# A two-layer hybrid encoder in fp32: bank layout of the prompt's Fourier mixing, and the engine that makes the weights' low parts

## The chip, the cores and the metric

The kernel runs on one core of a Trainium2 chip. The metric is the device time of one execution in microseconds; the number that counts is the median over runs. One launch computes both outputs.

## The reference

The same two layers and the same weights are applied to a prompt of 512 tokens and to a sample of 1024 tokens, all fp32, width 1024.

```python
for i in range(2):
    hn = rmsnorm(h, ln1[i])
    q, k, v, ga, uf, gf, mga, mgf = split(hn @ w_in[i])            # 1024 -> 4352 = 34 * 128
    a = band_attention(rope(q), rope(k), v, sink[i]) * silu(ga)    # 8 heads of 64, |i-j| <= 128
    f = fourier_mix(uf, w_fmix[i]) * silu(gf)
    merged = sigmoid(mga) * (a @ w_ao[i]) + sigmoid(mgf) * (f @ w_fo[i])
    h = h + merged @ w_out[i]
    gate = sigmoid(rmsnorm(h, ln_pg[i]) @ w_pg[i])
    h = h + (p[i] @ w_pe[i]) * gate
return rmsnorm(h, ln_f)

def fourier_mix(u, w):            # 4 channel groups of 128
    ug = u.reshape(B, S, 4, 128)
    f = real(fft2(ug, axes=(positions, group channels), norm="ortho"))
    return einsum("bsgc,gcd->bsgd", f, w)
```

## The kernel before

**Number format.** Every fp32 product is made of three products in fp32r. Each operand is split in two: ScalarE rounds it to the high part (L86, a cast), and the engine that `hi_lo` is given, VectorE (`V`) or GpSimd (`G`), subtracts it from the source for the low part (L87). `mm3` and `mm3_steps` then issue high by high (L98), high by low (L99) and low by high (L100) into one bank. So L86 and L87 occur all over the trace, and their groups are told apart by tile and shape.

**Stages of a layer.** The prompt is chunk 0, the sample chunks 1 and 2. `embed` (L625) makes `p @ w_pe` for all chunks. `project_prompt` (L489) multiplies the prompt by 34 weight tiles of 128 columns, 24 matmuls of 512 columns each; beside it `run` (L923) steps, at a rate written in the program, through the prompt's attention, `fourier(l, 0)` and the preparation of the sample. `project_pair` (L503) projects the sample in products of block sums (class `Pair`, matmuls on L233) beside the sample's attention. `merge(l, (0,), ...)` is the prompt's merge (branch outputs, output projection, gates), beside `fourier(l, 1)` for the sample; `merge(l, PAIR, ...)` is the sample's.

**Weights.** Class `Weights` (L148) holds a list of weight tiles. Each `get` hands out tile i, loads tile i + 3 from memory by the SyncE queue, and splits tile i + 2 in two halves of 128 x 512: `split` (L160) casts on ScalarE and subtracts on the engines in `engs`. The projection of layer 0's prompt has a list of its own, with both low parts on VectorE. From the sample's projection on, one list per layer serves everything (`streams(l)`): tiles 0 to 23 are the prompt's merge (8 for the branches, 8 output, 8 gates), the next 24 the sample's merge (16 and 8); behind these, in layer 0, stand the 34 tiles of layer 1's prompt projection, and in layer 1 the 8 gate tiles a second time, for chunk 2. All their low parts are GpSimd's.

**The prompt's Fourier part.** `fourier(l, 0)` folds the 512 positions of a channel group into two sets of 256 (`fold`, L790 on), for cosine and sine. For each set, and for even and odd positions apart, it multiplies by the channel transform (two matmuls, L854 of 256 columns and L855 of 128), into one bank each: misc, o, misc, misc. ScalarE copies one half of a bank to SBUF (L858), VectorE adds the other (L859), and the result is split again (L86, L87, 256 columns). One small product for the middle position takes an o bank. Then four sums over positions, of 128 columns (L98 to L100 into sc, sc, misc and misc), which a dozen small instructions of VectorE and ScalarE put together.

**Banks.** The eight banks of PSUM are pools: three mm, two sc, one o, two misc (`PS_BUFS`). Attention uses sc, o and misc; the norm's sums (L328) and its scale, transposed (L347 copies it out), use misc; projections and the prompt's merge use mm.

**What sets the order.** Each engine works its own instructions in the order of the program, and that order is not the one in which the source issues them: the program is built with a scheduler that simulates a timeline, so every edit moves instructions on all engines. `split` gives its tile's copies, and the release of a tile or a bank decides when the next one may be written.

**The end of a merge.** The sums of squares (L322, L323) go to TensorE (L328); the inverse root is twelve small VectorE steps (L332 to L339); TensorE transposes it, L347 copies it out, and L585 multiplies the first gate product by it and so empties its bank. With three mm banks TensorE can make three gate products before L585 has to be done.

## Time and profile before

| what | value |
|---|---|
| median of 3 runs | 2255.76 us (2255.22 to 2256.32) |
| the profiled execution, its own time | 2258.37 us |
| span of the profiled execution | 2255.9 us |
| mean granted clock of TensorE | 0.986 of full speed |
| TensorE, matmuls (PE) | 2182.3 us busy, 97% |
| VectorE (DVE) | 1460.9 us busy, 65% |
| ScalarE (ACT) | 1088.5 us busy, 48% |
| GpSimd (POOL) | 558.0 us busy, 25% |
| L87 on GpSimd, 128 x 512 | 284 instructions, 1448 ns each |
| L87 on VectorE, 128 x 512, from act | 290 instructions, 763 ns each |

All times are microseconds from the start of the span unless they say ns. A line number stands for a line of the kernel before. In the timeline, a bracket holds the idle time of the engine before the row, and the instruction that ended it; such a time is the gap between two busy times, and since matmuls overlap and their ends are modelled, starts are surer than ends. A granted clock of 1.00 is 2.4 GHz, one of 0.50 is 1.2 GHz. Names behind an operation are pools: `act` and `scr` in SBUF, `mm`, `sc`, `o` and `misc` in PSUM.

### The profile page before, as it was taken

Reading aid. Unit: us, or ns where it says so; the run is one execution under the profiler, and the core shown is the slowest. Engines: PE = TensorE matmul, PEld = TensorE weight load, DVE = VectorE, ACT = ScalarE, POOL = GpSimd, SP = SyncE. Lnnn points to the kernel's source line nnn. Section 1 sums busy time; section 2 is a strip of 40 time slices with the busy share of each in tenths; the row PEclk is TensorE's granted clock in tenths of the full one; section 3 lists DMA queues with packets and bytes.
Section 4 is the critical chain, followed back from the end, with each engine's and each line's share of the span. In section 5 each row is a group of like instructions: output and inputs, shape, how many; then the busy total and the mean of one; then the engine's idle time right before and its main releaser. Section 6 shows DMA issues by size and latency. Waiting matters only on the chain. (4 is left out here: it accounts for less than half of the span.)

```text
span 2255.9 us, 30026 instructions
## 1 busy us (share of the span) xinstructions
PE 2182.3 (97%) x10176; PEld 1809.5 (80%) x10176; DVE 1460.9 (65%) x2703; ACT 1088.5 (48%) x2340; POOL 558.0 (25%) x399
## 2 busy tenths in 40 slices
PE   8899999999999989999999999999999999999996
PEld 7777777788888878888888778787888888788885
DVE  5866657677667775464557564756766676864466
ACT  5477433466665454223324854336666644512342
POOL 0201100000004553312524253100000145641181
PEclk9899999999999999999999999999999999999998
DMA  7655544445448564731445554444444574653232
GB/s 279 230 181 167 188 140 163 148 137 166 150 133 294 189 236 174 251 103 51 146 158 188 173 178 167 151 165 137 143 141 158 194 270 159 225 201 117 83 118 98
DMA packets 240537, 380.69 MB, mean 169 GB/s; under 512 B 21120, under 2 KB 95488, under 8 KB 240384
## 3 DMA queue, kind: packets, MB, share of 16 engines
q1 hardware_dynamic: 233472, 366.19, 48.0%
q10 hardware_dynamic: 6912, 12.59, 1.5%
q8 instruction: 80, 1.31, 0.2%
q14 instruction: 73, 0.60, 0.1%
HBM read 270.17 MB, written 108.53 MB: 168 GB/s over the span
## 5 line engine op out<-in xcount | busy, mean ns | idle before, releaser
L233 PE MATMUL mm<-act,act 128*128 128x512 f32 x2856 | 695.2, 394 | 10.8 <-DVE scr L250 6.4
L233 PEld LDWEIGHTS mm<-act,act 128*128 128x128 f32 x2856 | 531.7, 188 | 123.4 <-issue 8.0
L98 PE MATMUL mm<-act,act 128*128 128x512 f32 x1408 | 559.1, 397 | 19.8 <-DVE scr L585 7.6
L100 PE MATMUL mm<-act,act 128*128 128x512 f32 x1408 | 556.5, 396 | 2.7 <-POOL act L87 1.3
L99 PE MATMUL mm<-act,act 128*128 128x512 f32 x1408 | 555.3, 394 | 0.0
L87 POOL TENSOR_TENSOR act<-act,act 128x512 fp32r<-128x512 f32 x284 | 404.1, 1448 | 547.2 <-ACT act L86 481.2
L86 ACT CAST act<-act 128x512 fp32r<-128x512 f32 x574 | 330.3, 619 | 225.1 <-DMA act<-in_w_af 60.7
L98 PEld LDWEIGHTS mm<-act,act 128*128 128x128 f32 x1408 | 267.8, 190 | 73.7 <-ACT act L86 13.0
L100 PEld LDWEIGHTS mm<-act,act 128*128 128x128 f32 x1408 | 267.5, 190 | 60.6 <-DVE act L87 3.5
L99 PEld LDWEIGHTS mm<-act,act 128*128 128x128 f32 x1408 | 268.1, 190 | 53.3
L87 DVE TENSOR_TENSOR act<-act,act 128x512 fp32r<-128x512 f32 x290 | 212.1, 763 | 47.1 <-ACT act L86 45.9
L87 DVE TENSOR_TENSOR act<-scr,act 128x512 fp32r<-128x512 f32 x256 | 193.7, 777 | 58.0 <-ACT act L86 56.3
L748 POOL TENSOR_TENSOR scr<-scr,scr 128x512 f32<-128x512 f32 x24 | 33.5, 1396 | 768.5 <-DVE scr L745 767.1
L86 ACT CAST act<-scr 128x512 fp32r<-128x512 f32 (+1 forms) x260 | 152.8, 615 | 144.4 <-DVE scr L410 69.0
L322 ACT ACTIVATE scr<-act 128x512 f32<-128x512 f32 x105 | 65.1, 631 | 233.7 <-DVE act L569 145.9
L87 DVE TENSOR_TENSOR act<-misc,act 128x512 fp32r<-128x512 f32 x132 | 88.1, 686 | 75.5 <-ACT act L86 75.1
L707 DVE CUSTOM_DVE_ANT_0 act<-sc,mask_sb,nsink_sb 128x384 f32<-128x384 f32 (+1 forms) x192 | 104.0, 569 | 46.4 <-PE sc L699 43.3
L710 ACT ACTIVATE act<-act,stat 128x385 f32<-128x385 f32 (+1 forms) x192 | 110.5, 578 | 43.9 <-DVE stat L707 43.4
L86 ACT CAST act<-misc 128x512 fp32r<-128x512 f32 x132 | 73.8, 586 | 106.8 <-PE misc L734 104.9
L98 PE MATMUL sc<-act,act 128*128 128x512 f32 (+1 forms) x292 | 111.1, 381 | 0.0
L100 PE MATMUL sc<-act,act 128*128 128x512 f32 (+1 forms) x292 | 110.6, 379 | 0.0
L99 PE MATMUL sc<-act,act 128*128 128x512 f32 (+1 forms) x292 | 110.5, 379 | 0.0
(207 smaller groups left out, 2642.8 us busy)
## 6 DMA issues: line engine op xcount, KB each, us to landing
act<-in_w_in SPq DMA_DIRECT2D x136, 256.0 KB, 4.5
act<-in_w_in SPq DMA_DIRECT2D x68, 512.0 KB, 4.8
gt<-scr SPq DMA_DIRECT2D x96, 256.0 KB, 2.3
scr<-gt SPq DMA_DIRECT2D x96, 256.0 KB, 5.3
act<-in_w_pg SPq DMA_DIRECT2D x80, 256.0 KB, 3.8
act<-in_w_af SPq DMA_DIRECT2D x64, 256.0 KB, 5.3
act<-in_w_out SPq DMA_DIRECT2D x64, 256.0 KB, 5.4
pl<-scr ACTq DMA_DIRECT2D x48, 256.0 KB, 2.5
```

The lines of the kernel that those rows point to most:

```text
L86: S.copy(hi, src)
L87: lo_eng.tensor_tensor(lo, src, f(hi), op=ALU.subtract)
L98: PE.matmul(out, wh, xh, start=i == 0, stop=False)
L99: PE.matmul(out, wh, xl, start=False, stop=False)
L100: PE.matmul(out, wl, xh, start=False, stop=i == n - 1)
L233: PE.matmul(bank, w, v, start=first and k == 0 and n == 0, stop=k == 3 and n == 2, skip_group_check=True)
L322: S.activation(sq, h, AF.Square)
L707: V.tensor_tensor_reduce(out=pr[:, :W], in0=sc[:, :W], in1=msk, scale=-0.125, scalar=nsink_sb[:, l, head : head + 1], op0=ALU.add, op1=ALU ...
L710: S.activation(pr, pr, AF.Exp, bias=nmx[:, e], scale=-1.0, accum_out=rs[:, e])
L748: G.tensor_tensor(a2, a2, gate, op=ALU.mult)
```

## The change

Three edits:

1. `split` picks its engines by the tile's number: tiles 0 to 23 of a layer's list and all from tile 48 on have both low parts on VectorE, tiles 24 to 47 stay with GpSimd. Layer 0's own projection list stays on VectorE throughout.
2. `embed` makes its first two halves of weights with a low part on VectorE, too, not on GpSimd.
3. `fourier(l, 0)`, the prompt's (s = 0), puts the sums of even and odd positions side by side in one misc bank, and one copy and one add empty it at 256 columns; the four sums go into two sc banks, two in each. The sample's Fourier part (s = 1) keeps its layout.

```diff
 # class Weights, split
-                for r, eng in zip((slice(0, 4), slice(4, 8)), self.engs):
+                for r, eng in zip((slice(0, 4), slice(4, 8)), self.engs[min(i // 24, 2)]):

 # embed
-                ws[k, i] = halves(raws[k][:, i, :], V if k else G)
+                ws[k, i] = halves(raws[k][:, i, :], V)

 # fourier: position sums of one channel group
                 for par in range(2):
-                    pm = pst(("misc", "o", "misc")[(2 * i + par) % 3])
+
+                    if s or par == 0:
+                        pm = pst(("misc", "o", "misc")[(2 * i + par) % 3] if s else "misc")
                     for t in range(n):
-                        j, lo = 2 * t * P, 2 * t * P + par
+                        j, lo = (2 * t if s else 2 * par) * P, 2 * t * P + par
                         uh, ul = (z[:, lo : lo + 2 * P - 1 : 2] for z in us[i])
                         PE.matmul(pm[:, j : j + 2 * P], uh, cw[i][:, :, gs], start=True, stop=False)
                         PE.matmul(pm[:, j : j + P], ul, cw[i][:, 0, gs], start=False, stop=True)
-                    pv = pm[:, : 2 * n * P].rearrange("p (t h d) -> p t h d", t=n, h=2)
-                    av = a[:, par * n * P : (par + 1) * n * P].rearrange("p (t d) -> p t d", t=n)
+                    if s == 0 and par == 0:
+                        continue
+                    pv = pm.rearrange("p (t h d) -> p t h d", t=2, h=2)
+                    av = (a[:, par * n * P : (par + 1) * n * P] if s else a).rearrange("p (t d) -> p t d", t=2)
                     S.copy(av, pv[:, :, 1])
                     V.tensor_tensor(av, av, pv[:, :, 0], op=ALU.add)

 # fourier: the four sums of one channel group
-            acc = [pst("sc"), pst("sc"), pst("misc"), pst("misc")]
+            if s:
+                acc = [pst("sc"), pst("sc"), pst("misc"), pst("misc")]
+            else:
+                b0, b1 = pst("sc"), pst("sc")
+                acc = [b0, b0[:, 2 * P :], b1, b1[:, 2 * P :]]

 # the program
-    ws = Weights(w_ins(0), (V, V))
+    ws = Weights(w_ins(0), ((V, V),) * 3)
...
-        ws = Weights(streams(l) + ([] if last else w_ins(l + 1)), (G, G))
+        ws = Weights(streams(l) + ([] if last else w_ins(l + 1)), ((V, V), (G, G), (V, V)))
```

In all 184 instructions move from GpSimd to VectorE, and 16 copies of ScalarE and 16 adds of VectorE go. The order on the engines changes with it, at two places above all. (Lines of the changed kernel are shifted: L856 there is L854 before, L857 is L855.)

TensorE, layer 0, the second channel group: before, from its third bank of position sums on, with the change from inside the block of both its banks on (misc and o are the position sums and the middle position, mm the projection, sc the four sums). Before:

```order
L854 MATMUL misc_2231<-act_1990,scr_2134 128x256
L855 MATMUL misc_2231<-act_1990,scr_2134 128x128
L98 MATMUL mm_2396<-act_462,act_2197 128x512
L99 MATMUL mm_2396<-act_462,act_2197 128x512
L100 MATMUL mm_2396<-act_462,act_2197 128x512
L98 MATMUL o_2251<-tiny_2137,act_1989 128x2
L99 MATMUL o_2251<-tiny_2137,act_1989 128x2
L100 MATMUL o_2251<-tiny_2137,act_1989 128x2
L854 MATMUL misc_2236<-act_1990,scr_2134 128x256
L855 MATMUL misc_2236<-act_1990,scr_2134 128x128
L98 MATMUL sc_2283<-act_1995,scr_2227 128x128
L99 MATMUL sc_2283<-act_1995,scr_2227 128x128
```

With the change:

```order
L100 MATMUL sc_2135<-act_1995,scr_2102 128x128
L98 MATMUL mm_2374<-act_344,act_2186 128x512
L857 MATMUL misc_2203<-act_1989,scr_2125 128x128
L856 MATMUL misc_2203<-act_1989,scr_2125 128x256
L857 MATMUL misc_2203<-act_1989,scr_2125 128x128
L857 MATMUL misc_2220<-act_1990,scr_2128 128x128
L856 MATMUL misc_2220<-act_1990,scr_2128 128x256
L857 MATMUL misc_2220<-act_1990,scr_2128 128x128
L99 MATMUL mm_2374<-act_344,act_2186 128x512
L100 MATMUL mm_2374<-act_344,act_2186 128x512
L98 MATMUL mm_2374<-act_358,act_2186 128x512
L99 MATMUL mm_2374<-act_358,act_2186 128x512
```

Before, the sums of the second set stood in pairs between the projection's matmuls, and the four sums followed the last pair at once. Now both sets stand in one block, with one bank for each set, and the projection's matmuls follow: 23 of them until the four sums (sc) begin.

VectorE, end of the prompt's merge in layer 0, from within the root steps (L337 to L339) to the first gate product (L585; L87 are low parts, from scr of the sample's merge, from act of weights and of the prompt). Before:

```order
L339 SCALAR_TENSOR_TENSOR tiny_7884<-misc_7879,tiny_7884 128x4
L337 TENSOR_TENSOR misc_7879<-misc_7879,tiny_7884 128x4
L338 SCALAR_TENSOR_TENSOR misc_7879<-misc_7879,tiny_7884 128x4
L339 SCALAR_TENSOR_TENSOR tiny_7884<-misc_7879,tiny_7884 128x4
L87 TENSOR_TENSOR act_7906<-act_7865,act_7906 128x512
L87 TENSOR_TENSOR act_7912<-act_7865,act_7912 128x512
L87 TENSOR_TENSOR act_7981<-scr_7915,act_7981 128x512
L87 TENSOR_TENSOR act_7986<-scr_7939,act_7986 128x512
L347 COPY scr_7960<-misc_7955 128x512
L585 TENSOR_TENSOR scr_7963<-mm_7843,scr_7960 128x512
L87 TENSOR_TENSOR act_8013<-scr_7941,act_8013 128x512
L587 SCALAR_TENSOR_TENSOR scr_7963<-scr_7963,scr_7962 128x512
```

With the change:

```order
L339 SCALAR_TENSOR_TENSOR tiny_7852<-misc_7847,tiny_7852 128x4
L87 TENSOR_TENSOR act_7874<-act_7833,act_7874 128x512
L87 TENSOR_TENSOR act_7877<-act_7827,act_7877 128x512
L87 TENSOR_TENSOR act_7880<-act_7833,act_7880 128x512
L87 TENSOR_TENSOR act_7888<-act_7802,act_7888 128x512
L87 TENSOR_TENSOR act_7891<-act_7802,act_7891 128x512
L87 TENSOR_TENSOR act_7949<-scr_7883,act_7949 128x512
L347 COPY scr_7928<-misc_7923 128x512
L87 TENSOR_TENSOR act_7954<-scr_7907,act_7954 128x512
L87 TENSOR_TENSOR act_7962<-act_7885,act_7962 128x512
L87 TENSOR_TENSOR act_7965<-act_7885,act_7965 128x512
L585 TENSOR_TENSOR scr_7931<-mm_7811,scr_7928 128x512
```

Among the steps ahead of L585 more low parts stand than before, since those of the weights are on this engine now.

## Rows read from the trace of the kernel before

**Rows 1.** Page, section 1: busy time, share of the span, instructions of each engine

```profile
PE 2182.3 (97%) x10176; PEld 1809.5 (80%) x10176; DVE 1460.9 (65%) x2703; ACT 1088.5 (48%) x2340; POOL 558.0 (25%) x399
```

**Rows 2.** Windows: stretch, us, PE, PEld, DVE, ACT, POOL busy, clock, DMA, GB/s

```profile
101.50:111.70 10.20, 6.54 (x15) 4.70 (x16) 9.45 (x16) 5.40 (x10) 0.00 (x0) 0.50 0.68 206
234.60:241.40 6.80, 6.80 (x24) 6.12 (x25) 4.56 (x23) 3.25 (x12) 0.59 (x1) 0.50 0.31 112
700.00:835.00 135.00, 129.34 (x664) 110.17 (x662) 102.42 (x184) 64.35 (x135) 78.53 (x55) 0.99 0.67 241
831.90:838.70 6.80, 3.46 (x8) 2.81 (x9) 5.88 (x9) 1.89 (x3) 1.32 (x1) 0.50 0.11 42
1200.00:1400.00 200.00, 192.57 (x930) 159.63 (x929) 115.00 (x256) 116.35 (x293) 85.74 (x64) 0.98 0.51 168
1340.50:1347.30 6.80, 6.36 (x17) 5.18 (x18) 3.31 (x15) 2.09 (x8) 2.07 (x3) 0.50 0.20 74
2000.00:2050.00 50.00, 50.00 (x222) 41.42 (x221) 25.22 (x35) 9.32 (x16) 10.59 (x8) 1.00 0.51 175
2197.20:2200.60 3.40, 3.40 (x9) 2.66 (x9) 1.50 (x13) 0.00 (x0) 0.00 (x0) 0.50 0.00 0
```

**Rows 3.** Timeline of TensorE, layer 0 Fourier; in brackets idle time before, releaser

```profile
214.49 0.39 PE L854 MATMUL misc<-act,scr 128*128 128x256 f32 x1 [0.93 <-DVE act L87]
...
224.52 0.39 PE L854 MATMUL o<-act,scr 128*128 128x256 f32 x1 [0.59 <-ACT scr L86]
...
234.60 0.58 PE L854 MATMUL misc<-act,scr 128*128 128x256 f32 x1 [2.76 <-DVE scr L859]
```

**Rows 4.** Timeline of TensorE, the prompt's Fourier part of layer 1

```profile
1319.27 0.39 PE L854 MATMUL misc<-act,scr 128*128 128x256 f32 x1 [0.93 <-DVE act L87]
...
1329.25 0.33 PE L855 MATMUL o<-act,scr 128*128 128x128 f32 x1 [0.66 <-DVE scr L87]
...
1339.23 0.33 PE L98 MATMUL misc<-act,scr 128*128 128x128 f32 x1 [1.11 <-ACT scr L86]
...
1340.94 0.69 PE L100 MATMUL misc<-act,scr 128*128 128x128 f32 x2 [1.06 <-DVE scr L87]
```

**Rows 5.** Timeline of VectorE, GpSimd and TensorE, end of the prompt's merge, layer 0

```profile
818.80 1.89 DVE L87 TENSOR_TENSOR act<-scr,act 128x512 fp32r<-128x512 f32 x3
...
820.30 12.91 POOL L87 TENSOR_TENSOR act<-act,act 128x512 fp32r<-128x512 f32 x8 [4.70 <-issue]
...
822.31 0.16 DVE L332 TENSOR_SCALAR misc<-misc 128x4 f32<-128x4 f32 x1
...
830.35 3.41 DVE L87 TENSOR_TENSOR act<-scr,act 128x512 fp32r<-128x512 f32 x2
...
834.40 0.69 DVE L585 TENSOR_TENSOR scr<-mm,scr 128x512 f32<-128x512 f32 x1
...
835.24 0.77 PE L98 MATMUL mm<-act,act 128*128 128x512 f32 x1 [5.90 <-DVE scr L585]
```

**Rows 6.** Groups by line and form: L86, L859, L858 at 256 columns

```profile
L86 ACT CAST scr<-scr 128x256 fp32r<-128x256 f32 x32 | 12.2, 405 | 17.0 <-DVE scr L859 9.8 <-DVE tiny L801 5.7 <-POOL scr L790 1.5
...
L859 DVE TENSOR_TENSOR scr<-scr,misc 128x256 f32<-128x256 f32 x24 | 9.6, 413 | 5.4 <-ACT scr L858 5.3
...
L858 ACT COPY scr<-misc 128x256 f32<-128x256 f32 x24 | 8.9, 372 | 33.6 <-PE misc L855 33.6
```

**Rows 7.** L87 on GpSimd, 1190 to 1400: ns least/median/most, and who waited

```profile
L87 POOL TENSOR_TENSOR act<-act,act x54: 1261/1297/1745, 1193.6 to 1388.8; 128x512 fp32r<-128x512 f32 x54
...
  PE mm L100: 1.3, 2
```

**Rows 8.** Timeline of TensorE, the prompt's projection in layer 0

```profile
104.04 0.76 PE L98 MATMUL mm<-act,act 128*128 128x512 f32 x1 [4.58 <-DVE scr L455]
...
106.35 0.80 PE L100 MATMUL mm<-act,act 128*128 128x512 f32 x1 [1.12 <-DVE act L87]
```

**Rows 9.** Timeline of TensorE, the last norm's sums in layer 1

```profile
2194.47 1.92 PE L328 MATMUL misc<-mean_sb,scr 128*128 128x1 f32 x16 [1.39 <-DVE scr L323]
```

## The prediction

> **What bounds the kernel now.** I read the page first, then the windows by stage, then the timeline of the engine that binds. TensorE is busy for 97% of the span [rows 1], so only two things can be won: stretches in which TensorE stands idle, and stretches in which it runs at half clock. The windows show the second [rows 2]: the granted clock is 0.50, the lower of the two levels (1.2 GHz), for 6.8 us at 234.6, 6.8 us at 831.9, 6.8 us at 1340.5 and 3.4 us at 2197.2; elsewhere, as at 2000, it is 1.00 and 222 matmuls pass in 50 us, 0.225 us each. A stretch of 6.8 us at half clock does the work of 3.4 us, so each such stretch costs at most 3.4 us.
>
> The timeline of TensorE shows what stands before each of these drops. In layer 0 the prompt's Fourier part stalls TensorE for 0.93, 0.59 and 2.76 us, and the clock falls at the end of the last stall [rows 3]. In layer 1 the same part stalls it for 0.93, 0.66, 1.11 and 1.06 us (two shorter ones are not counted), and the clock falls at 1340.5, between the last two [rows 4]. At the end of the prompt's merge in layer 0 it stands for 5.90 us [rows 5], and the clock falls within that. All of these end with VectorE or ScalarE: a bank that has not been emptied, or a low part that has not been made.
>
> Why VectorE is late there is in the same rows. While GpSimd works through eight low parts in 12.91 us, two of VectorE's own take 3.41 us; when GpSimd was idle for most of the time, three took 1.89 us, 0.63 each [rows 5]. So a low part of GpSimd's does not come free: it holds up VectorE by about 1.1 us (3.41/2 - 0.63), which is more than VectorE would need to do that low part itself.
>
> **The change, part by part.**
>
> *A. Prompt's Fourier part, layer 0.* A channel group took four banks for the position sums (three misc, one o) and four for the four sums (two sc, two misc). It now takes two misc and two sc; o is left to the middle position alone. The 2.76 us stall is the third misc bank of a group, waiting for the first to be emptied by L859; the 0.59 one waits for a high part, with TensorE already at an o bank of the next group. The order shows the new run: all eight matmuls of the position sums stand together, and 23 matmuls of the projection (5.2 us) stand before the sums that use them. That is longer than the chain they wait for: copy 0.37, add 0.41, high part 0.41, and a low part that I price as the add, 1.6 us together [rows 6]. I let 0.59 and 2.76 go: 3.3 us. The 0.93 us stall waits for a low part of the weight table (L87) and stays. The half-clock stretch follows an idle TensorE; without the stall I take it to go as well, 3.4 us (bounds 0 and 3.4). The matmuls are the same in number and shape. Sixteen copies and sixteen adds fewer in both layers together lie on ScalarE and VectorE, beside TensorE's work: nothing on the path.
>
> *B. The same in layer 1.* Of 0.93, 0.66, 1.11 and 1.06 us the first stays, 2.8 us go. Here GpSimd leaves as well: of its low parts between 1190 and 1400, 54 in all [rows 7], only the few before the next layer's weights remain. The half clock at 1340.5: 3.4 us, same bounds.
>
> *C. End of the prompt's merge, layer 0.* TensorE's fourth gate product needs the bank that L585 empties, and L585 waits for the norm's chain, which started at 822.31 with L332 and ended with L585 at 835.09: 12.8 us [rows 5]. In the new order eleven low parts stand in that chain instead of six, because the weights' come to VectorE, but GpSimd has none of its own there. Eleven at 0.63, twelve short steps at 0.16, the copy L347 and L585 at 0.69 each: 10.2 us, 2.6 less. Three matmuls fewer stand between the norm's sums and the transposes (0.7 us), so TensorE arrives sooner and gains 1.9 us of the 5.90. Bounds: 0, if ScalarE's high parts are late, and 5.90. About 4 us of idle time remain, longer than the 2.76 in A before which the clock fell, so I leave the half clock in place. In layer 1 the chain has few low parts and TensorE's own transposes set it: nothing.
>
> *D. The whole merge as a load.* Between 700 and 835 VectorE is busy for 102.4 of 135 us and GpSimd for 78.5 [rows 2]. Of the 55 instructions of GpSimd some 40 move, 25 us at 0.63; they give back up to 1.1 each where they collided. VectorE does not become the bound: at most 128 of 135 us even if nothing came back.
>
> *E. Layer 1's projection.* Its 34 weight tiles move as well, 68 low parts, since every tile from the 48th of a stream on is VectorE's. TensorE's waits for GpSimd there, 1.3 us [rows 7], go. Against this VectorE gets up to 54 x 0.63 = 34 us more in 200 us of which 115 are busy [rows 2]. Layer 0 already works in this way, and there TensorE lost 4.58 and 1.12 us to VectorE's backlog [rows 8], and 10.2 us at half clock [rows 2], 5.1 lost: 10.8 together. In layer 0 that followed two norm copies and twelve pinned products in one block; in layer 1's new order these are spread between products. I charge 2.2 us, nearer to nothing (bounds 0 and 10.8).
>
> *F. The last gates.* 16 low parts move to VectorE, whose steps were held up. The last norm's sums waited 1.39 us for L323 [rows 9], and 3.4 us at half clock followed [rows 2], 1.7 lost: 3.1 us go (bounds 0 and 3.1).
>
> *G. New stalls in the Fourier part.* Eight groups get a new order, and its gaps come out on the chip, not on paper. Bounds: nothing, and one stall like the 1.11 in each group, 8.9 us. I charge 3.0, since most places have over 20 matmuls of cover. The two low parts of the first weights go to VectorE, where it was idle. No DMA is added, removed or moved past another queue's.
>
> Sum: 3.3 + 3.4 + 2.8 + 3.4 + 1.9 + 1.3 + 3.1 = 19.2, less 2.2 and 3.0: **14.0 us**. The sum is made in the profiled execution of 2258.4 us, 2.6 us above the median of the runs, 2255.8; taken from the median it gives **2241.8 us**.
>
> *A rule against the change.* A bank with two sums can be emptied only when both are done; before, the copy of the even half could start while TensorE wrote the odd half in another bank. The Trainium skill ("PSUM — Partial Sum Buffer", Summary: rules for kernel authors) says that whoever reads a bank during matmuls should have them write a different bank. No row of this trace shows two halves in one bank. By the rule the overlap is lost; by the order TensorE has other work meanwhile, so the sum stands.
>
> **Rivals.**
>
> 1. *The half clock stays* in A, B and F, because the stretches have small matmuls enough to bring it about without a stall. For it: at 1340.5 the stalls beside it are short. Against: elsewhere the same small matmuls run at full clock. 8.5 us less gained: 2250.3.
>
> 2. *VectorE's backlog moves into layer 1's projection* as in layer 0, 10.8 instead of 2.2: 2250.4, and up to 2255 if the Fourier part behind it stalls too. For it: the same lines wait in layer 0. Against: 115 of 200 us leave room.
>
> 3. *Slower: the shared bank serialises.* If TensorE stands through the chain of 1.6 us after each of the 16 shared banks of position sums (eight groups, two each), that is 25.6 us, in place of today's 8.0 us of stalls; the half clock stays, and only C, E and F (6.3) help: 2255.8 + 25.6 - 8.0 - 6.3 = 2267.1. It decides where fewer than seven projection matmuls (1.6/0.225) stand between a bank's last matmul and its use. For it: all sums of a group stand in one block now. Against: the order shows 23.
>
> 4. *The change does little*: the low parts leave GpSimd, but ScalarE's high parts set the waits: 2254.
>
> **How the numbers follow.** My forecast has 0.64, rival 1 0.17, rival 2 0.12, rival 3 0.05, rival 4 0.02. About 0.2% (4.5 us) is what a measurement of this kernel can tell from no change. Faster by more, under 2251.3: all of the forecast, 0.12 of rival 1, 0.06 of rival 2: 0.82. Within 0.2%: the rest of 1 and 2, and rival 4: 0.13. Slower: rival 3: 0.05. Range: if all stalls of rows 3 to 5, 7 and 9 went (4.3 + 3.8 + 5.9 + 1.3 + 1.4) and all half clock (11.9), 28.6 us, 2227; I start at 2228. Upwards it takes in rivals 1 and 2 in the main: 2253.
>
> **What would show it.** Right: VectorE's L87 at 0.68 all through the merge; no stall over 1.2 us in either prompt's Fourier part and no half clock there; the stall before L585 at some 4 us. Wrong: a clock of 0.50 still near 235 or 1340 (rival 1), stalls on L455 or L707 near 1240 (rival 2), stalls on the sums' low parts in each group (rival 3), or GpSimd's share unchanged.

## The result and the profile after

The changed kernel took **2236.76 us** in the median of four runs (2235.67 to 2243.05), beside 2255.49 us for the kernel before: a ratio of 0.9923, with a 95% interval of 0.9904 to 0.9942. A second comparison (change_again, below) gave 0.9921 (0.9908 to 0.9933). So the change is faster by some 17.5 us. The prediction said 2241.8 us and a range of 2228 to 2253.

The page's first section, with columns as in [rows 1] (PE and PEld are TensorE's matmuls and weight loads, DVE is VectorE, ACT ScalarE, POOL GpSimd):

```profile
PE 2171.5 (97%) x10176; PEld 1803.0 (81%) x10176; DVE 1503.1 (67%) x2871; ACT 1088.7 (49%) x2324; POOL 297.8 (13%) x215
```

The number of matmuls is the same; GpSimd lost 260 us of work and VectorE gained only 42, though 184 low parts came to it. The windows of the changed kernel, columns as in [rows 2]: the two prompt Fourier parts (210.7 and 1304.1), the prompt's merge (690) and layer 1's projection (1187), and two of the stretches that are left at half clock (823.2 and 1307.9).

```profile
210.70:244.10 33.40, 32.75 (x184) 27.82 (x183) 25.28 (x84) 20.14 (x58) 8.54 (x9) 1.00 0.71 236
...
823.20:826.60 3.40, 3.40 (x9) 2.65 (x8) 2.58 (x5) 1.26 (x2) 0.00 (x0) 0.50 0.21 78
1304.10:1339.60 35.50, 33.92 (x182) 28.85 (x181) 24.44 (x84) 19.40 (x54) 5.13 (x4) 0.95 0.55 186
1307.90:1311.30 3.40, 3.40 (x9) 2.62 (x10) 3.40 (x13) 2.42 (x6) 0.00 (x0) 0.50 1.07 316
690.00:825.00 135.00, 131.64 (x671) 112.13 (x670) 112.91 (x226) 65.79 (x136) 24.84 (x16) 0.99 0.67 241
1187.00:1387.00 200.00, 196.38 (x959) 163.85 (x958) 130.31 (x307) 118.50 (x290) 15.72 (x12) 0.99 0.53 175
```

The same two Fourier parts in the kernel before:

```profile
212.50:260.40 47.90, 43.16 (x212) 36.22 (x211) 27.08 (x97) 21.84 (x67) 10.15 (x10) 0.93 0.52 176
1317.30:1363.50 46.20, 41.67 (x205) 34.67 (x204) 28.35 (x82) 21.07 (x63) 22.42 (x18) 0.93 0.48 159
```

In layer 0 TensorE's idle time fell from 47.90 - 43.16 = 4.7 us to 0.65 and the clock rose from 0.93 to 1.00. In layer 1 idle time fell from 4.5 to 1.6, but one piece at half clock (1307.9) is left, where there were 6.8 us [rows 2]. The timeline of TensorE has no stall over 0.7 us in either part; these rows answer to [rows 3, 4], and the next two to [rows 5, 9]:

```profile
212.65 0.39 PE L856 MATMUL misc<-act,scr 128*128 128x256 f32 x1 [0.34 <-DVE act L87]
...
1325.20 0.70 PE L856 MATMUL misc<-act,scr 128*128 128x256 f32 x2 [0.67 <-ACT scr L86]
...
822.46 0.47 PE L98 MATMUL mm<-act,act 128*128 128x512 f32 x1 [3.36 <-DVE scr L585]
...
2174.09 1.92 PE L328 MATMUL misc<-mean_sb,scr 128*128 128x1 f32 x16 [0.41 <-DVE scr L323]
```

VectorE's chain before the 3.36 us stall, which answers to [rows 5]:

```profile
812.37 0.17 DVE L332 TENSOR_SCALAR misc<-misc 128x4 f32<-128x4 f32 x1
...
815.61 3.10 DVE L87 TENSOR_TENSOR act<-act,act 128x512 fp32r<-128x512 f32 x5
...
821.63 0.69 DVE L585 TENSOR_TENSOR scr<-mm,scr 128x512 f32<-128x512 f32 x1
```

Five low parts take 3.10 us, 0.62 each, where two took 3.41 beside GpSimd [rows 5]. From L332 to the end of L585 it is 9.95 us.

**Where the time went.** The profiled executions took 2258.37 and 2235.67 us, 22.7 apart; their spans are 22.0 apart, and these are followed here. The stages run from one mark to the next. A mark is the same matmul in both traces: the first of 128x256 in a Fourier part, L328 of a norm, or the first L233 of a layer. A stall right before a mark belongs to the stage ahead of it.

| stage | before, mark to mark | after | gain |
|---|---|---|---|
| start to layer 0's Fourier part | 214.49 | 212.65 | 1.8 |
| layer 0's Fourier part to the sample's projection | 86.69 | 77.51 | 9.2 |
| sample's projection and most of the prompt's merge | 519.11 | 520.57 | -1.5 |
| end of that merge, sample's merge | 263.83 | 260.69 | 3.1 |
| rest of it, layer 1's projection | 235.15 | 234.69 | 0.5 |
| layer 1's Fourier part to the sample's projection | 86.50 | 80.33 | 6.2 |
| sample's projection to the last gates | 738.58 | 738.29 | 0.3 |
| last gates and end | 111.53 | 109.16 | 2.4 |

Some of the small numbers are a few matmuls that stand on the other side of a mark. The 1.8 us at the start are the clock's (13.6 us at half clock before, 6.8 after); in a second trace of the changed kernel they are 0.6. The brackets over 0.1 us in TensorE's timeline, behind its first matmul, sum to 55.3 us before and 43.8 after, 11.5 less. The mean granted clock gives about the other half: 2255.9 x (1 - 0.986) = 31.6 us were lost to the clock before, and 2233.9 x (1 - 0.991) = 20.1 after, 11.5 less, good to some 2 us because the clock has three digits. By the stretches at 0.50 (62 us before, 42 after) it is 10 less.

### The profile page after: what moved, and what is told of

Read it like the earlier page. It is cut to its first block, busy times and chain, and to the rows that moved or that the text cites. A ratio compares the mean times of both kernels' runs of the same rounds, so it can differ in the third digit from the quotient of the medians.

```text
span 2233.9 us, 29956 instructions
## 1 busy us (share of the span) xinstructions
PE 2171.5 (97%) x10176; PEld 1803.0 (81%) x10176; DVE 1503.1 (67%) x2871; ACT 1088.7 (49%) x2324; POOL 297.8 (13%) x215
## 3 DMA queue, kind: packets, MB, share of 16 engines
q1 hardware_dynamic: 233472, 366.19, 48.5%
## 5 line engine op out<-in xcount | busy, mean ns | idle before, releaser
L233 PE MATMUL mm<-act,act 128*128 128x512 f32 x2856 | 697.4, 394 | 10.3 <-DVE scr L250 6.0
L233 PEld LDWEIGHTS mm<-act,act 128*128 128x128 f32 x2856 | 532.1, 189 | 123.2 <-ACT act L86 8.0
L98 PE MATMUL mm<-act,act 128*128 128x512 f32 x1408 | 555.4, 395 | 18.4 <-ACT act L86 7.6
L100 PE MATMUL mm<-act,act 128*128 128x512 f32 x1408 | 553.2, 393 | 1.5 <-DVE act L87 1.3
L86 ACT CAST act<-act 128x512 fp32r<-128x512 f32 x574 | 329.8, 619 | 211.6 <-DMA act<-in_w_af 61.3
L87 DVE TENSOR_TENSOR act<-act,act 128x512 fp32r<-128x512 f32 x474 | 331.8, 734 | 40.1 <-ACT act L86 38.7
L98 PEld LDWEIGHTS mm<-act,act 128*128 128x128 f32 x1408 | 266.1, 189 | 71.5 <-ACT act L86 12.9
L100 PEld LDWEIGHTS mm<-act,act 128*128 128x128 f32 x1408 | 266.2, 189 | 58.2 <-DVE act L87 3.9
L87 DVE TENSOR_TENSOR act<-scr,act 128x512 fp32r<-128x512 f32 x256 | 181.0, 728 | 53.3 <-ACT act L86 52.0
L86 ACT CAST act<-scr 128x512 fp32r<-128x512 f32 (+1 forms) x260 | 152.8, 615 | 131.0 <-DVE scr L410 68.8
L87 POOL TENSOR_TENSOR act<-act,act 128x512 fp32r<-128x512 f32 x100 | 142.9, 1454 | 324.2 <-ACT act L86 305.8
L87 DVE TENSOR_TENSOR act<-misc,act 128x512 fp32r<-128x512 f32 x132 | 88.2, 686 | 74.3 <-ACT act L86 73.9
L86 ACT CAST act<-misc 128x512 fp32r<-128x512 f32 x132 | 73.9, 587 | 105.7 <-PE misc L734 103.9
L98 PE MATMUL sc<-act,act 128*128 128x512 f32 (+1 forms) x292 | 110.8, 379 | 0.0
L100 PE MATMUL sc<-act,act 128*128 128x512 f32 (+1 forms) x292 | 110.1, 378 | 0.0
```

Of the source, the lines that this page charges most:

```text
L86: S.copy(hi, src)
L87: lo_eng.tensor_tensor(lo, src, f(hi), op=ALU.subtract)
L98: PE.matmul(out, wh, xh, start=i == 0, stop=False)
L100: PE.matmul(out, wl, xh, start=False, stop=i == n - 1)
L233: PE.matmul(bank, w, v, start=first and k == 0 and n == 0, stop=k == 3 and n == 2, skip_group_check=True)
```

## The experiments

Each kernel's time at full clock, its span times its mean granted clock, separates work and stalls from what the clock costs (the clock has three digits, so each is good to about 1 us). The split is not clean: where TensorE is slowed ahead of a stall, the stall shrinks, as engines_only shows below. The table has medians over the runs, and the sum of TensorE's brackets over 0.1 us of one trace, behind its first matmul. Each ratio is taken to runs of the kernel before in the same comparison; its row gives the range over four of these.

| kernel | median us (runs) | ratio to before | span x clock | lost to the clock | idle |
|---|---|---|---|---|---|
| before, four comparisons | 2256.9 to 2257.6 (50) | 1 | 2223.3 to 2225.8 | 29.3 to 31.6 | 55.3 |
| the change, first | 2236.8 (4) | 0.9923 (0.9904 to 0.9942) | 2212.6 | 23.5 | 43.8 |
| change_again | 2240.9 (5) | 0.9921 (0.9908 to 0.9933) | 2213.7 | 24.6 | 44.5 |
| banks_only | 2245.7 (6) | 0.9951 (0.9938 to 0.9964) | 2217.9 | 25.8 | 46.4 |
| engines_only | 2246.2 (9) | 0.9963 (0.9951 to 0.9976) | 2216.5 | 29.2 | 46.0 |
| even_odd_only | 2245.9 (4) | 0.9953 (0.9938 to 0.9968) | 2216.8 | 28.0 | 48.2 |
| four_sums_only | 2248.4 (9) | 0.9964 (0.9953 to 0.9975) | 2218.0 | 29.2 | 48.5 |
| merge_tiles_pool | 2239.7 (4) | 0.9925 (0.9912 to 0.9939) | 2216.1 | 23.5 | 44.8 |
| late_tiles_pool | 2241.0 (4) | 0.9930 (0.9916 to 0.9944) | 2215.3 | 24.6 | 45.0 |
| all_vector | 2244.3 (5) | 0.9944 (0.9930 to 0.9957) | 2216.6 | 26.9 | 50.4 |
| short_cover_new | 2257.0 (10) | 1.0005 (0.9995 to 1.0014) | 2220.1 | 33.8 | 50.5 |
| short_cover_old | 2270.4 (4) | 1.0063 (1.0048 to 1.0079) | 2228.6 | 40.8 | 55.0 |
| later_sample | 2236.4 (5) | 0.9913 (0.9900 to 0.9925) | 2212.3 | 22.3 | 43.6 |
| spread_sample | 2232.6 (4) | 0.9888 (0.9871 to 0.9904) | 2210.5 | 18.9 | 42.4 |

### The two parts apart

banks_only takes the changed kernel and gives every low part back to the engine that had it:

```diff
-                ws[k, i] = halves(raws[k][:, i, :], V)
+                ws[k, i] = halves(raws[k][:, i, :], V if k else G)
-        ws = Weights(streams(l) + ([] if last else w_ins(l + 1)), ((V, V), (G, G), (V, V)))
+        ws = Weights(streams(l) + ([] if last else w_ins(l + 1)), ((G, G),) * 3)
```

> Only the Fourier edit; every low part where it was before. Theory: the bank layout alone removes the stalls of the prompt's Fourier part in both layers and the half clock behind them, about 15 of the 19 us: 2239 to 2243 us, no stall over 1.2 us in either part, GpSimd still at some 558 us busy. Rival (GpSimd's low parts hold VectorE up, and that is why banks were emptied late): the layout alone gives little, 2250 us or more, and stalls of over 1 us stay in layer 1's part, where GpSimd works beside it.

Measured: 2245.65 us, between the ranges of the theory and the rival. Layer 0's part is as in the change (no stall over 0.4 us, no half clock). In layer 1's, with GpSimd busy beside it for 21.8 of 35 us, these stalls and 6.8 us at half clock are left:

```profile
1331.24 0.33 PE L100 MATMUL sc<-act,scr 128*128 128x128 f32 x1 [0.62 <-DVE scr L87]
...
1333.86 0.47 PE L857 MATMUL misc<-act,scr 128*128 128x128 f32 x1 [0.71 <-DVE scr L87]
```

engines_only is the kernel before with the engine choice in `split` and the embedding alone, the Fourier part untouched.

> Only the low parts move (weights and embedding); the Fourier part keeps its banks. Theory: it gains at the end of layer 0's prompt merge (about 3 us) and at the last gates (about 2.4 us) alone, 2248 to 2251 us, and the 2.76 us stall of layer 0's Fourier part and its half clock stay. Rival: the low parts carry most of the gain, 2244 us or less.

Measured: 2246.16 us, between the two again. The stall at the merge's end is 3.35 us, as in the change, and that of the last norm 0.5. Unforeseen, layer 1's Fourier part gained as well: its idle time in the old layout is 2.1 us of 43 where it was 4.5. GpSimd works beside it for only 6.8 us now, where it was 22.4; the order of the matmuls there changed, too. VectorE's low parts and L859 in this part, before (1317.3 to 1363.5) and then in engines_only (1311 to 1354); the mean of one in ns stands ahead of the second bar:

```profile
L87 DVE TENSOR_TENSOR scr<-scr,scr 128x256 fp32r<-128x256 f32 x13 | 9.3, 737 | 3.2 <-ACT scr L86 3.0
L859 DVE TENSOR_TENSOR scr<-scr,misc 128x128 f32<-128x128 f32 x11 | 3.0, 281 | 8.4 <-ACT scr L858 8.3
...
L87 DVE TENSOR_TENSOR scr<-scr,scr 128x256 fp32r<-128x256 f32 x13 | 6.2, 496 | 1.1 <-ACT scr L86 0.7
L859 DVE TENSOR_TENSOR scr<-scr,misc 128x128 f32<-128x128 f32 x12 | 3.4, 283 | 5.6 <-ACT scr L858 5.5
```

In layer 0 the theory missed: 6.8 us at half clock stayed, but the 2.76 us stall did not, though banks and order around it are those of before:

```profile
232.93 0.40 PE L854 MATMUL misc<-act,scr 128*128 128x256 f32 x1
```

The half clock came earlier here, from 222.7 on. From the sums in the o bank (222.82) to these it took 10.1 us, as before (224.52 to 234.60): TensorE made the matmuls between them more slowly and arrived when VectorE was done. So a stall and a half clock ahead of it did not add up here.

The two ratios multiply to 0.9914, the change's within the intervals: about 11 us for the banks and 8 for the engines. **That they add is not shown.** At full clock the parts are worth 6.9 and 8.3 us apart and 9.6 together (change_again and its own comparison), and idle time falls by 8.9 and 9.3 apart and 11.5 together. They overlap, in layer 1's Fourier part for one, where either alone brings the idle time from 4.5 us to some 2 and both to 1.6.

### Which half of the bank edit

even_odd_only puts the four sums back, four_sums_only the position sums:

```diff
 # even_odd_only
-                acc = [b0, b0[:, 2 * P :], b1, b1[:, 2 * P :]]
+                acc = [pst("sc"), pst("sc"), pst("misc"), pst("misc")]
 # four_sums_only
-                    if s or par == 0:
-                        pm = pst(("misc", "o", "misc")[(2 * i + par) % 3] if s else "misc")
+                    pm = pst(("misc", "o", "misc")[(2 * i + par) % 3])
```

> The changed kernel with the four sums back in sc, sc, misc, misc; even and odd positions still share a bank. Theory: the third misc bank of a group was the stall, so this half carries the gain: 2237 to 2241 us. Rival: the four sums' two misc banks hold up the next group's position sums, and a stall of 1 to 3 us per layer comes back there: 2243 to 2248 us.

> The changed kernel with the position sums back in misc, o, misc, misc, each emptied by itself; the four sums in two sc banks. Theory: the third misc bank of a group still waits for the first to be emptied, 2243 to 2249 us with a stall on L859's successor. Rival: it was the four sums in misc that kept the misc banks busy, and without them the old position sums run free: 2237 to 2241 us.

Measured: 2245.94 and 2248.43 us. Both stand beside engines_only (2246.16), the change without any bank edit: **neither half alone can be told from nothing (at full clock 2216.8 and 2218.0 us beside 2216.5, with more idle time), and both together are worth the 0.42% between 0.9963 and 0.9921.** The first theory fell and its rival held; of the second the time held, but not the place. TensorE's stalls in layer 0, first of even_odd_only, then of four_sums_only:

```profile
229.58 0.33 PE L98 MATMUL sc<-act,scr 128*128 128x128 f32 x1 [1.20 <-ACT scr L86]
...
233.55 0.48 PE L98 MATMUL misc<-act,scr 128*128 128x128 f32 x1 [2.25 <-ACT scr L86]
```

```profile
224.96 0.58 PE L854 MATMUL misc<-act,scr 128*128 128x256 f32 x1 [0.75 <-ACT scr L86]
...
236.23 0.33 PE L98 MATMUL sc<-act,scr 128*128 128x128 f32 x1 [1.28 <-ACT scr L86]
```

All wait for a high part, no longer for a bank. In three of the four it is that of position sums, which were made too shortly before their use; at 224.96 it is that of the folded prompt, ahead of the position sums. The order of matmuls around one group (P position sums, m projection, M middle, S the four sums; counts from the traces) says why:

```
before           P2(o)  m20  P2 m1 P2 m3 M3  [2.76 idle]  P2  S
even_odd_only    S6(misc)  m21  P4 m1 P4 m2 M3  [1.20 idle]  S
four_sums_only   m19  P1 m5 P2 M3  S  [1.28 idle]  S
the change       P2 S4 m1 P6  m23  S
```

A group's position sums can run ahead of the block of projection matmuls only if all their banks are free by then. In even_odd_only the misc banks still hold the four sums of the group before; in four_sums_only there are only three banks for four position sums. So the last of them slides behind the block of some 20 matmuls, and the chain copy, add, high part, low part is left uncovered. Only with both halves do the position sums have the two misc banks to themselves. This account is read from the orders and the pools.

### The two halves of the engine edit, and the rest of the tiles

In all three the change's `((V, V), (G, G), (V, V))` is altered: merge_tiles_pool has `(G, G)` first, late_tiles_pool last, all_vector has `(V, V)` throughout.

> The changed kernel with tiles 0 to 23 (the prompt's merge) back on GpSimd. Theory: the stall before L585's successor at the end of layer 0's prompt merge goes from 3.4 back to 5.9 us and nothing else changes, since TensorE had no other stall in that merge: 2 to 4 us slower than the change, 2239 to 2242. Rival: VectorE, held up by GpSimd all through the merge, sets more than its end: 2245 or more.

> The changed kernel with all tiles from 48 on (layer 1's projection, the last gates) back on GpSimd. Theory: the last norm's sums wait 1.4 instead of 0.4 us again with 3.4 us at half clock behind them, and layer 1's projection waits 1.3 us for GpSimd: 2 to 4 us slower than the change, 2239 to 2242. Rival (VectorE's backlog in layer 1's projection costs as much as GpSimd's delays): 0 to 1 us slower.

> The changed kernel with the remaining tiles 24 to 47 (the sample's merge) on VectorE as well. Theory: in the sample's merge TensorE has no stall but the one before L585's successor in layer 1 (1.8 us), and VectorE has room, so the time stays within 3 us of the change: 2234 to 2240. Rival A: VectorE, with four norms and gates beside, becomes late and TensorE stalls in the sample's merge: 2242 or more. Rival B: the weights' low parts are ready sooner and the 1.8 us stall shrinks: 2232 to 2234.

Measured: 2239.69, 2240.98 and 2244.33 us. The two stalls that were named first came back as forecast, first of merge_tiles_pool, then of late_tiles_pool:

```profile
825.60 0.76 PE L98 MATMUL mm<-act,act 128*128 128x512 f32 x1 [5.87 <-DVE scr L585]
```

```profile
2177.77 1.47 PE L328 MATMUL misc<-mean_sb,scr 128*128 128x1 f32 x12 [1.40 <-DVE scr L323]
```

The rest of late_tiles_pool's forecast did not: no half clock followed its stall, and layer 1's projection waits 0.35 us for GpSimd, not 1.3. The times cannot be told from the change's (intervals overlap almost wholly). At full clock they stand some 2 to 3 us above it, about the size of these stalls. all_vector was slower as rival A had it (its interval and the change's still overlap a little), yet not where rival A looked: the sample's merge has no new stall, but the final norm's sums, behind the last gates, wait 13.27 us where they wait 6.51 in the change. The first of these rows is VectorE's last step ahead of the last norm's sums, the other two are TensorE's; the fourth is from the change:

```profile
2173.10 0.69 DVE L323 TENSOR_TENSOR scr<-scr,scr 128x512 f32<-128x512 f32 x1 [0.70 <-ACT scr L322]
...
2179.49 1.84 PE L328 MATMUL misc<-mean_sb,scr 128*128 128x1 f32 x16
...
2223.12 0.34 PE L328 MATMUL misc<-mean_sb,scr 128*128 128x1 f32 x1 [13.27 <-DVE scr L323]
```

```profile
2217.82 0.34 PE L328 MATMUL misc<-mean_sb,scr 128*128 128x1 f32 x1 [6.51 <-DVE scr L323]
```

VectorE is ready for the last norm's sums at 2173.8, as in the change (2173.9). But the sums begin at 2179.49 and not at 2174.09, with no wait: 30 more gate matmuls stand ahead of them in TensorE's order (121 behind them, up to the final norm, where the change has 151). VectorE's steps behind them all come 5.3 us later, and TensorE has 30 matmuls less to cover them with. So it was no low part that cost the time, but the place of these sums in the order, which moved with the edit.

### The same kernel twice

> The changed kernel once more, unedited, for a second trace and a narrower interval. Theory: the stalls of TensorE are set by the order of the program, so its idle time of over 0.1 us adds up to the same 44 us within 1 us, while the half-clock stretches come in pieces of 3.4 us whose places are partly chance: their cost (14.6 us in the first trace) may differ by 2 to 5 us, and with it the time. Rival: the half clock follows from the stalls, and its stretches stand at the same places to within a piece. Both expect a ratio to before of 0.990 to 0.994.

Measured: 2240.89 us. Idle time is 44.5 us (43.8), but the clock cost 26.9 us (20.1). By the stretches at 0.50, 42 us in the first trace and 52 in the second, the difference is some 5 us, and the 14.6 us that were expected to stand for the first trace are too few. The theory held: 29 of 36 stalls are the same to a tenth of a microsecond, the half clock is not. The largest exception is in layer 1's Fourier part, the same instruction as at 1325.20 above, now with 6.8 us at half clock from 1326.4 on:

```profile
1326.52 0.89 PE L856 MATMUL misc<-act,scr 128*128 128x256 f32 x2 [1.88 <-ACT scr L86]
```

Why that high part was 1.2 us later in this execution stays open.

### Without cover

To see when the shared bank does cost something, short_cover_new and short_cover_old step the prompt's Fourier part twice as fast, in the changed kernel and in the one before:

```diff
+    def twice(g):
+        for _ in g:
+            next(g, None)
+            yield
...
-            (chain(attention(l, (0,), False), fourier(l, 0), pair_made(xs, l, range(2, 3))), 4 * MT_U + 4, 2.1),
+            (chain(attention(l, (0,), False), twice(fourier(l, 0)), pair_made(xs, l, range(2, 3))), 4 * MT_U + 4, 2.1),
```

> The changed kernel with the prompt's Fourier part stepped twice as fast, so that its work stands closer together. By the order, four of the eight groups then have 0 to 2 projection matmuls between their position sums and the four sums that use them, where the change has 7 to 25. Theory (the cover is what makes the shared bank free): TensorE stalls for 1 to 2 us in each of those four groups, 5 to 9 us idle in the two Fourier parts against 2 to 3 in the change, and 3 to 7 us at half clock: 2243 to 2250 us. Rival (fewer banks and copies are enough, cover or not): at most 3 us idle there, 2236 to 2241.

> The kernel before with the prompt's Fourier part stepped twice as fast in the same way. Theory: it stalls as well, as often as the order leaves its sums uncovered and at the third misc bank of a group besides, 10 us idle or more in the two Fourier parts, 2254 to 2264 us; the new layout is better at little cover, too. Rival (with little cover the separate banks overlap and the shared one does not): fewer stalls than the changed kernel at the same pace.

Measured: 2257.0 and 2270.4 us, both above the ranges of their theories. The whole gain of the change is gone at short cover, but most of that is not the shared bank's: the new layout stays 13 us ahead of the old at the same pace, and the old one loses 13.5 us by it, too. At full clock the pace costs the new layout 6.4 to 7.5 us and the old one 4.1, so some 3 us may be put down to the shared bank, near what the times at full clock can tell. Stalls stand in the groups without cover, in TensorE's timeline of short_cover_new; the first stands in the middle position's product, the other two before the four sums:

```profile
215.52 0.37 PE L99 MATMUL o<-tiny,act 128*128 128x2 f32 x1 [1.12 <-DVE tiny L801]
...
241.53 0.33 PE L98 MATMUL sc<-act,scr 128*128 128x128 f32 x1 [1.35 <-ACT scr L86]
...
1347.13 0.33 PE L98 MATMUL sc<-act,scr 128*128 128x128 f32 x1 [0.71 <-ACT scr L86]
```

The windows of its two Fourier parts, columns as in [rows 2]:

```profile
210.00:257.00 47.00, 40.12 (x188) 32.73 (x187) 33.43 (x106) 23.36 (x66) 13.91 (x11) 0.85 0.46 153
1318.00:1356.00 38.00, 35.30 (x167) 29.97 (x166) 30.07 (x103) 21.94 (x61) 8.56 (x6) 0.78 0.50 164
```

Idle are 6.9 us in layer 0, 2.2 of them behind the Fourier part, and 2.7 in layer 1; without those 2.2 it is 7.4, within the theory's 5 to 9 (11.3 in short_cover_old, as its theory had it). The time went beyond it by the clock. In layer 1 no stall is over 0.71 us, and still the clock is 0.78: the half clock came there without a long stall, while the prediction had it that the stall brings it. What brings it is not shown. The same few small matmuls open layer 0's part in the changed kernel (from 211.9 on, with gaps of 0.21 and 0.34 us), and there the clock stays at 1.00.

### A version that beats both

The two stalls of 4.58 and 1.12 us before L98 and L100 in layer 0's projection [rows 8] are there in the change, too (4.58 at 102.75, 1.33 at 105.05), with 6.8 us at half clock from 103.0 on. They are VectorE's backlog of twelve products for the sample.

later_sample begins that work later and slower, spread_sample spreads it evenly and moves the attention back:

```diff
 # later_sample
-            (pair_made(xs, l, range(2)), 24, 1.0),
+            (pair_made(xs, l, range(2)), 24 if l else 34, 1.0 if l else 0.3),
 # spread_sample
-            (pair_made(xs, l, range(2)), 24, 1.0),
-            (chain(attention(l, (0,), False), fourier(l, 0), pair_made(xs, l, range(2, 3))), 4 * MT_U + 4, 2.1),
+            (pair_made(xs, l, range(2)), 24 if l else 30, 1.0 if l else 0.6),
+            (chain(attention(l, (0,), False), fourier(l, 0), pair_made(xs, l, range(2, 3))), 4 * MT_U + 4 + (0 if l else 12), 2.1),
```

> The changed kernel with the preparation of the sample in layer 0 begun at step 34 instead of 24 of the prompt's projection and at a rate of 0.3 instead of 1.0, so that VectorE has four of the sample's products ahead of the first L455 and not twelve. The orders of both prompt Fourier parts on TensorE stay word for word. Theory: the two stalls near 103 us (4.6 and 1.3 us) are VectorE's backlog of those products; they shrink by 3 to 6 us and the half clock behind them by up to 3.4: 2229 to 2235 us, 4 to 8 under the change. Rival: the products are only moved, the backlog meets the next L455 or attention and the time is that of the change within 2 us.

> The changed kernel with the preparation of the sample in layer 0 spread over steps 30 to 56 of the prompt's projection (rate 0.6), and the prompt's attention begun 12 steps later, so that what is left of the preparation is not run off at one go at step 44. Theory: the 5.7 us stall at 127 us of the run before came from that run-off (a weight's high part behind the sample's products on ScalarE); with the work spread, neither it nor the two stalls near 103 us come back, 5 to 6 us less idle than in the change and 1 to 3 us less half clock: 2229 to 2234 us. Rival: the work meets the attention instead, and TensorE stalls there by as much: 2236 to 2241.

Measured: 2236.38 us for later_sample, its rival's case. The two stalls went, and at step 44, where the rest is run off at one go, this one came:

```profile
127.09 0.80 PE L98 MATMUL mm<-act,act 128*128 128x512 f32 x1 [5.67 <-ACT act L86]
```

spread_sample took **2232.59 us** (0.9888, 0.9871 to 0.9904), below both intervals of the change; its own ends where the first of them begins. At full clock it is 2210.5 us beside 2212.6 and 2213.7, and lost to the clock are 18.9 beside 23.5 and 24.6, so a good part of the gain is the clock's. The same 17 us of the changed kernel and of spread_sample, in windows:

```profile
95.00:112.00 17.00, 11.09 (x37) 8.09 (x37) 16.25 (x27) 6.00 (x11) 0.00 (x0) 0.80 0.48 157
```

```profile
95.00:112.00 17.00, 17.00 (x77) 14.08 (x76) 16.50 (x27) 6.54 (x13) 0.00 (x0) 1.00 0.37 124
```

Twice the matmuls pass in the same time, with VectorE as busy as before. But most of it was given back elsewhere, in part in the Fourier parts (idle 1.9 us in layer 0 and 3.2 in layer 1, against 0.65 and 1.6): over the whole trace the idle time is 42.4 us, 1.4 to 2.1 below the change's two traces and not 5 to 6 as the theory had it.

## Why the prediction was right, step by step

- **A, layer 0's Fourier part: right, sized too small.** 6.7 us were forecast and 9.2 came: 4.1 of stalls, 3.4 for the half clock, and 1.7 that are neither. The 2.76 and 0.59 us stalls went, and two shorter ones that were not counted. The 0.93 one, which was to stay, fell to 0.34 (it stands ahead of the mark and is not in the 9.2). The half clock went as supposed: in all eight traces with both bank edits at the old pace there is none in this part; in the four others at that pace (before, engines_only, even_odd_only, four_sums_only) there is, beside stalls of 0.59 to 2.76 us. That the stall alone decides is not shown: spread_sample has one of 1.07 us there and no half clock. The covered chain behind 23 matmuls, read from the order, is what happened. That the four sums' move out of misc is needed for it was not seen: the step put it on "the third misc bank of a group", and even_odd_only shows that this bank alone is not the cause.
- **The half clock elsewhere: misread.** The prediction had a clock of 1.00 outside the four stretches that it named. But its [rows 2] has 0.50 at 101.5, too, and the trace before also has it at 81.0, 340.4, 1528.2 and from 2238.2 to the end: 62 us in all, of which it priced 23.8.
- **B, layer 1: the stalls right, the clock not.** 2.8 us of stalls were forecast, 2.9 came (4.5 to 1.6). Of the 3.4 us for the half clock, the first trace had half and the second nothing: 6.2 us of gain in the one, 82.9 us from mark to mark and so 3.6 in the other. Rival 1 (the half clock stays) holds in this layer: all eight traces with both bank edits at the old pace have 3.4 or 6.8 us of it here. The reason it gave, small matmuls without a stall, is not shown: the drop at 1307.9 has stalls of 0.34 and 0.35 us right before it, and four_sums_only has 2.5 us idle in this part and no half clock. In the second trace the sign of a right forecast, no stall over 1.2 us, fails as well (1.88).
- **C, end of the merge: right.** 10.2 us of chain were forecast, 9.95 measured; 1.9 us of stall were to go, 2.5 did. The stall follows the engine of the merge's tiles in all fourteen traces: 5.87 to 6.32 us in the four with GpSimd, 3.35 or 3.36 in nine of the others and 3.86 in spread_sample. The half clock was to stay at 6.8 us; 3.4 stayed in both traces of the change, 6.8 in four others with these tiles on VectorE.
- **D: right.** VectorE's busy time in the merge rose from 102.4 to 112.9 of 135 us, under the bound of 128, as 184 more instructions cost it 42 us over the span. With GpSimd busy for 24.8 us there and not for 78.5, the rest came back to VectorE, and TensorE saw it only at the places named.
- **E: the backlog did not come.** A loss of 0.9 us was the balance; 0.5 were gained. Rival 2 is out: the brackets over 0.1 us in TensorE's timeline from layer 0's last norm sums to layer 1's Fourier part sum to 2.0 us in both traces.
- **F: right in kind.** 2.4 us instead of 3.1: the wait is 0.41 us (0.89 in the second trace), and the half clock went in both. That it went with the stall is luck: late_tiles_pool has a stall of 1.40 us there and no half clock behind it, later_sample one of 0.87 and 3.4 us.
- **G: charged too much.** 3.0 us for new stalls; 0.35 and 0.67 us came in the first trace, 0.35 and 1.88 in the second, all in layer 1, and they are in B's measured gain already.
- **The rule against the change** (bank read only when both sums are done) cost nothing to be seen at the change's cover. Where the order leaves none (short_cover_new) the stalls on position sums are 0.5 to 1.35 us, less than the 1.6 of rival 3. The gain is gone there, but the old layout loses nearly as much by the same pace, so rival 3 is not shown to be the reason.

By medians the sum missed by 5 us. In the profiled executions, in which it was made, the gain was 22.0 against 14.0: of the 8.0 us A has 2.5, G's charge 3.0, E 1.4 and C's stage 1.2, F takes back 0.7, and the other 0.6 lie in stages that were priced at nothing. The execution profiled after the change is the fastest of its four. The times of one kernel differ by up to 7 us from run to run (2235.55 to 2242.66 in change_again), at the same time at full clock (2213.7 and 2214.0), so a part of the good fit is luck.

## What to carry to other kernels

Where two kinds of sums share a pool of PSUM banks, look at which of them must be made before the block of work that is to cover its evacuation, and count in the order how many matmuls stand between a sum and its use: freeing the bank of one may be worth nothing until the other has moved, too. For differences of a few microseconds, split each time into span times granted clock and the rest; the first is the steadier (but see engines_only, where a half clock hid a stall). On an engine with slack, look for lumps of early work before taking work away: spreading one brought another 0.3% here, in part by the clock.

## What was not expected

- The half clock needs no long stall. The Trainium skill ("TensorE: Matmul & The Clock Gate", Why this matters for your kernels) asks for no long idle gaps between bursts. No gap over 0.7 us stands near 1321.3 in short_cover_new, and yet 10.2 us at half clock began there, behind matmuls of 2 to 256 columns with gaps of 0.13 to 0.67 us. So keeping to that advice did not keep the clock up here.
- Two executions of one program differed by some 5 us in what the clock cost, at almost the same stalls.
- GpSimd's low parts were probably worth taking away for VectorE's sake in layer 1's Fourier part, too: 4.5 to 2.1 us idle with the old banks. The Trainium skill ("SBUF — State Buffer", Who interferes with whom) has it that a VectorE instruction with two SBUF inputs contends with a GpSimd instruction that reads SBUF. The 0.62 us of a low part alone and 1.7 beside GpSimd [rows 5] agree, and so do the rows of engines_only: L87, with both inputs in SBUF, took 737 ns before and 496 there, L859, with one of them in PSUM, 281 and 283.
